# A second branch's gates by Strassen's seven products in a two-layer hybrid trunk, with the output projection's halves swapped

## The chip, the cores and the metric

One core of one Trainium2 chip runs the whole program. The metric is the time of one execution on the device in microseconds (us), the median of several runs. The engines are named as in the profile: PE is TensorE's matmuls and PEld its weight loads, DVE is VectorE, ACT is ScalarE, POOL is GpSimd, SP is the engine that issues most DMAs.

## What is computed

Two layers over 256 tokens of 1,024 features, all in fp32. The part of a layer that matters here is the mixer and its merge (`u` is the normalised input, 256 x 1024; `y_a`, `y_b`, `y_c` are the outputs of the pooling, convolution and attention branches, 256 x 512 each):

```python
u = rms_norm(h, norm_mix_g[i])
proj = u @ w_in[i]
a_in, c_x, c_b, c_c, q, k, v, gates = jnp.split(proj, split_at, axis=-1)
...
g_a, g_b, g_c = jnp.split(jax.nn.sigmoid(gates), N_BRANCHES, axis=-1)
merged = (g_a * (y_a @ w_pool_out[i])
          + g_b * (y_b @ w_conv_out[i])
          + g_c * (y_c @ w_attn_out[i]))
h = h + merged @ w_o[i]
```

Each of the three gates is a product of `u` with 1024 x 1024 columns of `w_in`. After the merge come a squared-ReLU MLP (1024 to 4096 and back) and a gated per-layer embedding.

## The kernel before

**Weights.** All weights stream from memory once, in a fixed order that `weight_plan` (line 93) writes out. A unit is 128 x 1024 fp32. `WeightStream.prefetch` (line 274) turns each unit into two parts: ScalarE rounds it to fp32r (`whi`, line 285) and VectorE subtracts that from the original (`wlo`, line 286). A product is then three matmuls: high by high, high by low, low by high. Splits run up to `AHEAD = 5` units ahead of the unit in use, in six buffers of parts. Plain loads go through three staging tiles of two units (1 MB each), issued by SP at line 250, in the order of the plan.

**Kinds of units around the change.** An A unit (`unit_a`, line 416) covers 256 rows of weights by 512 columns for both halves of the tokens: 12 matmuls of 512 columns (line 425). An S unit (`unit_s`, line 439) is half of one of Strassen's products: 6 matmuls of 512 columns (lines 444, 446, 448). A gate of 1024 x 1024 takes 8 A units, or seven products of 2 S units.

**Strassen's products.** They need sums of quarters of the weights. These are made in two tiles of 1 MB, `sums`, which come from the four-buffer pool `t8`: two plain loads by SP (line 233), one VectorE add of 128 x 2048 (line 265, after product 1 is split), and three DMAs from POOL that add to what lies there (line 256: after products 1, 5 and 6 are split). Products 1, 5, 6, 4 read the first tile, 7 the second; 2 and 3 use plain weights through the staging tiles. `sums_busy` stops all further loading at the next product 1 until product 4 is split. The token side needs four sums and differences of the input, made and split by `token_sums` (line 917) at the places in `TOKEN_SUMS_AT`.

**Sums of products.** Products 1, 6, 7, 4 add up in one bank of PSUM ("chain"), 5 and 3 in another ("five"), 2 in a third ("two"). Before the next product adds to a bank, its present content must be read out: after 1, 5 and 6 by a ScalarE copy (`copied`, line 960), after 7 by a VectorE add (line 965). VectorE adds and ScalarE sigmoids (line 970) give the four quarters of the gate. Before, this is done for branch A's gates (`GATED = 0`) and for two groups of the MLP's second product (`GROUPS`).

**The order.** `merge_order` (line 43) writes out the order of the merge: `g` are A units of a gate, `p` those of a branch's output projection, `S` a product. Side work is attached to a unit with `at(u, ...)` and emitted right after it; `u_b` is the last unit of the conv columns, so the merge starts at `u_b + 1` and has 42 units. A merge (line 996) multiplies a projection by its sigmoid (line 999) and adds it up (line 1003); when all three branches of a half of the features are in, `merge_t` transposes it (line 496) and splits it (lines 517, 518) into the operand of `w_o`. The first half is complete after `p(0, 0)`, the second after `p(0, 1)`; `w_o` (8 A units) takes the low half first. The tile framework orders each engine's instructions when it compiles, by program position and by the times that it assumes; on the chip every engine runs its list in order.

**Side work of the merge.** Attention's end, the pooling branch (windows, `pool_map`), and the convolution: `conv` (line 887) is one VectorE multiply (line 892) and two multiply-adds (line 895) for each of four groups, `conv_gate` (line 898) two multiplies and two splits.

Of the kernel before, what the change touches and what calls it, by code (L numbers as in the profile page):

```python
# [36 lines left out]
GATED = 0  # L37

TOKEN_SUMS_AT = (8, 9, 10, 12, 14, 17)
# [3 lines left out]
def merge_order():  # L43

    def g(br, f, *which):
        return [("g", br, f, ((0, 2), (4, 6))[n]) for n in which]

    def p(br, f):
        return [("p", br, f)]

    def prod(n):
        return [("S", n)]
# [40 lines left out]
def weight_plan():  # L93
# [12 lines left out]
    for i in range(DEPTH):  # L106
# [15 lines left out]
        for kind, *what in merge_order():  # L122
            if kind == "S":
                plan.extend(("S", what[0], i, k, "gate") for k in (0, 2))
# [25 lines left out]
def quarter(i, j, h, f):  # L150

    if j == "gate":
        return tuple(("A", "w_in", i, 4 * h + k, GATE + GATED * D + 512 * f) for k in (0, 2))
    return tuple(("A", "w_down", i, 4 * (j + h) + k, 512 * f) for k in (0, 2))
# [21 lines left out]
def weight_blocks():  # L176

    place = {}
    for _, block in transfer_plan():
        if block:  # L180
            place.setdefault(block, len(place))
    for i in range(DEPTH):
        for j in ("gate", *GROUPS):
            place.setdefault(quarter(i, j, 0, 1), len(place))
    return place


class WeightStream:
# [30 lines left out]
    def load(self, parts=1, between=None):  # L219


        while self.next_dma < len(self.transfers):
# [3 lines left out]
            if own and prod == 1:  # L226
# [3 lines left out]
                if j == "gate" or j == GROUPS[0]:  # L230
# [79 lines left out]
def kernel(  # L310
# [224 lines left out]
    for i in range(DEPTH):  # L535
# [344 lines left out]
        for n in range(4):  # L880
            at(u_b - 3 + n, window, n)
# [3 lines left out]
        at(u_b + 6, pool_map, 1)  # L885

        def conv(g):
# [4 lines left out]
            nc.vector.tensor_scalar_mul(out=yv[:, g, :], in0=zp[:, g, PAD:], scalar1=cw[2])  # L892
# [56 lines left out]
        def gate_product(n, k):  # L949
# [6 lines left out]
            unit_s(get(("acc", SUM[n])), *parts, n, i, k, "gate", n not in (1, 5, 2))  # L956
# [5 lines left out]
        def gate_sum(t, f, bank, n):  # L962
# [3 lines left out]
            sigmoid(t, f, v, v)  # L966

        def sigmoid(t, f, src, out):
            sig[GATED, t, f] = out
# [3 lines left out]
        def gate_product_out(n):  # L973
            gops.pop(n, None)
            if n in (1, 5):
                copied(n)
            elif n == 6:
                copied(6)
                gate_sum(0, 1, tiles.pop(("acc", "five")), 6)
            elif n == 7:  # L980
                gate_sum(1, 1, tiles[("acc", "chain")], 5)
                gops.pop(("s", 5))
            elif n == 2:
                gate_sum(0, 0, tiles.pop(("acc", "two")), 1)
            elif n == 4:
                sigmoid(1, 0, tiles.pop(("acc", "chain")), t2())

        def merge_key(br, f):
            return ("bpair", "p", br, f) if br else ("p", br, f)
# [15 lines left out]
        def merge_t(f):  # L1005
            if f == 0:
# [11 lines left out]
        for kind, *what in merge_order():  # L1018
            if kind == "S":
                for k in (0, 2):  # L1020
                    u = add(gate_product, what[0], k)
                if what[0] != 3:
                    at(u, gate_product_out, what[0])
# [342 lines left out]
```

## Time and profile before

| | before |
|---|---|
| median of 3 runs | 843.99 us (843.08 to 844.75) |
| profiled execution | 843.23 us, of which the span of the instructions is 841.4 us |
| PE busy | 834.1 us (99%) |
| DVE busy | 661.3 us (79%) |
| ACT busy | 547.6 us (65%) |
| DMA moved | 177.32 MB, mean 211 GB/s |

The profile lists for each engine its instructions with start and length; a busy share is over the span. Matmuls are pipelined: each is listed for some 0.39 us, but the next starts 0.23 us later, so their cost is read from their starts. Lengths of VectorE and ScalarE instructions also overlap a little; in a row of several alike, the whole over the count is the cost of one.

### The profile page before, as it was taken

How to read it: one execution, taken by the hardware profiler on the slowest of the kernel's cores; microseconds unless marked ns; L12 is line 12 of the kernel's file. 1: busy time of each engine (PE TensorE's matmuls, PEld its weight loads, DVE VectorE, ACT ScalarE, POOL GpSimd, SP SyncE). 2: the span in 40 equal slices, each digit the busy share in tenths (PEclk: the TensorE clock that was granted, in tenths of full speed). 3: DMA queues.
4: the chain of work that ended last, by engine and by line, in shares of the span. 5: the costliest groups of instructions: out<-in, count | busy, mean ns of one | idle time of the engine just before them, and what ended most of it. 6: DMA issues, size and time to landing. Idle time of an engine off the chain costs nothing.

```text
span 841.4 us, 11683 instructions
## 1 busy us (share of the span) xinstructions
PE 834.1 (99%) x4492; PEld 721.0 (86%) x4492; DVE 661.3 (79%) x910; ACT 547.6 (65%) x789; POOL 47.8 (6%) x52
## 2 busy tenths in 40 slices
PE   9999999999999999999999999999999999999997
PEld 7999988888988888888879998888889888888886
DVE  5987889976689677977678777998766886789864
ACT  6755566654688667976665645666546876688662
POOL 2400000000000000000022000000000000000000
PEclk9999999999999999999999999999999999999999
DMA  9864649754658766866445546486555767669531
GB/s 336 311 223 150 226 123 274 231 208 170 270 172 262 244 239 181 261 192 221 179 168 194 191 166 234 129 246 226 211 190 225 246 211 254 243 199 248 192 133 51
DMA packets 27127, 177.32 MB, mean 211 GB/s; under 512 B 3136, under 2 KB 4032, under 8 KB 6464
## 3 DMA queue, kind: packets, MB, share of 16 engines
q1 hardware_dynamic: 24192, 157.53, 50.5%
q0 software_dynamic: 2592, 18.88, 11.8%
q8 instruction: 35, 0.57, 0.3%
q10 hardware_dynamic: 288, 0.18, 0.1%
q14 instruction: 20, 0.16, 0.1%
HBM read 175.52 MB, written 1.05 MB: 210 GB/s over the span
## 4 chain that ended last, share of the span: by engine, by line
PE 98%; DMA 0%; ACT 0%; issue 0%; DVE 0%; SPq 0%
PE acc L425 38%; PE bp L473 12%; PE bp L475 6%; PE bp L425 6%; PE bp L464 5%; PE bp L462 5%; PE bp L460 5%; PE acc L446 3%; PE acc L448 3%; PE acc L444 3%; PE acc L436 3%; PE bp L448 2%; PE bp L446 2%; PE bp L444 2%; PE tr L496 1%; PE acc L1280 1%
## 5 line engine op out<-in xcount | busy, mean ns | idle before, releaser
L286 DVE TENSOR_TENSOR wlo<-stage,whi 128x1024 fp32r<-128x1024 f32 (+1 forms) x272 | 328.4, 1213 | 121.7 <-ACT whi L285 120.1
L285 ACT CAST whi<-stage 128x1024 fp32r<-128x1024 f32 (+1 forms) x272 | 282.7, 1044 | 205.4 <-PE acc L425 82.7
L425 PE MATMUL acc<-whi,t 128*128 128x512 f32 x928 | 298.7, 393 | 0.0
L425 PEld LDWEIGHTS acc<-whi,t 128*128 128x128 f32 x928 | 173.5, 188 | 35.1 <-ACT whi L285 0.4
L425 PE MATMUL acc<-wlo,t 128*128 128x512 f32 x464 | 180.9, 390 | 0.0
L473 PE MATMUL bp<-t,whi 128*128 128x512 f32 x448 | 122.3, 394 | 0.0
L425 PEld LDWEIGHTS acc<-wlo,t 128*128 128x128 f32 x464 | 87.2, 188 | 17.5 <-DVE wlo L286 0.2
L460 PE MATMUL bp<-t,whi 128*128 128x256 f32 x320 | 90.7, 284 | 0.0
L464 PE MATMUL bp<-t,wlo 128*128 128x256 f32 x320 | 90.5, 283 | 0.0
L462 PE MATMUL bp<-t,whi 128*128 128x256 f32 x320 | 90.5, 283 | 0.0
L473 PEld LDWEIGHTS bp<-t,whi 128*128 128x128 f32 x448 | 77.7, 189 | 11.3
L286 DVE TENSOR_TENSOR wlo<-t,whi 128x1024 fp32r<-128x1024 f32 x60 | 72.9, 1220 | 14.8 <-ACT whi L285 13.8
L285 ACT CAST whi<-t 128x1024 fp32r<-128x1024 f32 x60 | 62.9, 1052 | 29.1 <-PE acc L425 11.4
L475 PEld LDWEIGHTS bp<-t,wlo 128*128 128x128 f32 x448 | 68.8, 189 | 9.4
L475 PE MATMUL bp<-t,wlo 128*128 128x256 f32 x448 | 71.5, 281 | 0.0
L462 PEld LDWEIGHTS bp<-t,whi 128*128 128x128 f32 x320 | 61.1, 191 | 0.4
L460 PEld LDWEIGHTS bp<-t,whi 128*128 128x128 f32 x320 | 61.0, 191 | 0.4
L464 PEld LDWEIGHTS bp<-t,wlo 128*128 128x128 f32 x320 | 61.1, 191 | 0.1
L256 POOL DMA_DIRECT2D t<-in_w_dram x18 | 15.9, 884 | 477.4 <-ACT t L1116 192.7
L446 PE MATMUL acc<-wlo,t 128*128 128x512 f32 x104 | 40.6, 390 | 0.0
L448 PE MATMUL acc<-whi,t 128*128 128x512 f32 x104 | 40.5, 390 | 0.0
L444 PE MATMUL acc<-whi,t 128*128 128x512 f32 x104 | 40.5, 390 | 0.0
(176 smaller groups left out, 1057.9 us busy)
## 6 DMA issues: line engine op xcount, KB each, us to landing
stage<-in_w_dram SPq DMA_DIRECT2D x131, 1024.0 KB, 4.8
t<-in_w_dram POOLq DMA_DIRECT2D x18, 1024.0 KB, 8.5
t<-in_w_dram SPq DMA_DIRECT2D x12, 1024.0 KB, 6.4
stage<-in_w_dram SPq DMA_DIRECT2D x6, 512.0 KB, 5.3
stage<-in_w_dram SPq DMA_DIRECT2D x4, 256.0 KB, 4.7
h<-in_x_dram SPq DMA_DIRECT2D x4, 256.0 KB, 9.9
t<-in_xT_dram SPq DMA_DIRECT2D x1, 512.0 KB, 7.6
out_dram<-h SPq DMA_DIRECT2D x2, 256.0 KB, 2.0
```

The costliest lines, as they stand in the source:

```text
L285: self.nc.scalar.copy(out=hi[:, cs], in_=src[:, cs])
L286: self.nc.vector.tensor_sub(out=lo[:, cs], in0=src[:, cs], in1=hi[:, cs].bitcast(F32))
L425: nc.tensor.matmul(accs[t], lhsT=lhs[:, kx + j, tk], rhs=rhs[:, j, :], start=begins[t] and j == 0 and n == 0, stop=last and j == 1 and n == 2,
L436: nc.tensor.matmul(accs[half][t], lhsT=lhs[:, k, t * P:(t + 1) * P], rhs=rhs[:, 0, cs], start=k == 0 and n == 0, stop=False)
L444: nc.tensor.matmul(bank, lhsT=xh[:, k + n, :], rhs=wh[:, n, :], start=first, stop=False, skip_group_check=True)
L446: nc.tensor.matmul(bank, lhsT=xh[:, k + n, :], rhs=wl[:, n, :], start=False, stop=False, skip_group_check=True)
L448: nc.tensor.matmul(bank, lhsT=xl[:, k + n, :], rhs=wh[:, n, :], start=False, stop=k + n == 3, skip_group_check=True)
L460: nc.tensor.matmul(bp[:, m, :], lhsT=wh[:, j, ms], rhs=xh[:, kx + j, :], start=first, stop=False, skip_group_check=True)
L462: nc.tensor.matmul(bp[:, m, :], lhsT=wh[:, j, ms], rhs=xl[:, kx + j, :], start=False, stop=False, skip_group_check=True)
L464: nc.tensor.matmul(bp[:, m, :], lhsT=wl[:, j, ms], rhs=xh[:, kx + j, :], start=False, stop=last, skip_group_check=True)
L473: nc.tensor.matmul(bank, lhsT=wh[:, k, :], rhs=xk[k], start=k == 0, stop=False, skip_group_check=True)
L475: nc.tensor.matmul(bank[:, 1, :], lhsT=wl[:, k, :], rhs=xk[k][:, 0, :], start=False, stop=k == KD - 1, skip_group_check=True)
```

## The change

Branch B's gates (`g_b`) are computed by the seven products too, behind those of A and in the same two tiles of weight sums. Eight A units of B's gates per layer become fourteen S units. The token sums are made earlier, and their splits are kept until B's products have used them. The four gate units of C and the products of A now come first; `conv` and `conv_gate` move seven units back, and the first operation of `conv` moves from VectorE to ScalarE. All projections use a pair of banks of the pool `bp`. The second half of the features is now complete first, after `p(1, 1)`; the first half waits for product 4 of B, so the projection `p(1, 0)` stays in its two banks until then. `w_o` takes the high half first.

```diff
-GATED = 0
-TOKEN_SUMS_AT = (8, 9, 10, 12, 14, 17)
+GATED = (0, 1)
+TOKEN_SUMS_AT = (6, 7, 8, 9, 10, 15)
...
-    def g(br, f, *which):
-        return [("g", br, f, ((0, 2), (4, 6))[n]) for n in which]
+    def g(f, *which):
+        return [("g", 2, f, ((0, 2), (4, 6))[n]) for n in which]
...
-    order = g(2, 0, 0, 1) + g(2, 1, 0, 1) + p(2, 0) + prod(1) + p(2, 1) + prod(5) + g(1, 0, 0) + prod(3)
-    order += g(1, 0, 1) + prod(6) + p(1, 0) + prod(7) + g(1, 1, 0) + prod(2) + g(1, 1, 1) + prod(4)
-    return order + p(0, 0) + p(1, 1) + p(0, 1)
+    order = g(0, 0, 1) + prod(0, 1) + g(1, 0) + prod(0, 5) + g(1, 1) + prod(0, 3) + p(2, 0) + prod(0, 6) + p(2, 1)
+    order += prod(0, 7, 2, 4) + p(0, 0) + prod(1, 1) + p(0, 1) + prod(1, 5, 3) + p(1, 0)
+    return order + prod(1, 6, 7) + p(1, 1) + prod(1, 2, 4)
...
-        for ks in (low, high):
+        for ks in (high, low):
             for f in range(2):
                 a("w_o", ks, f * 512)
...
-                if j == "gate" or j == GROUPS[0]:
+                if j == "gate0" or j == GROUPS[0]:
                     self.sums = self.new_sums()
...
-            nc.vector.tensor_scalar_mul(out=yv[:, g, :], in0=zp[:, g, PAD:], scalar1=cw[2])
+            nc.scalar.activation(out=yv[:, g, :], in_=zp[:, g, PAD:], func=AF.Copy, scale=cw[2])
...
-            at(u_b + 15 + g, conv, g)
+            at(u_b + 22 + g, conv, g)
         for m in range(2):
-            at(u_b + 20 + m, conv_gate, m)
+            at(u_b + 27 + m, conv_gate, m)
...
-        def gate_product_out(n):
-            gops.pop(n, None)
+        def gate_product_out(br, n):
+            if br == GATED[-1]:
+                gops.pop(n, None)
...
-            return ("bpair", "p", br, f) if br else ("p", br, f)
+            return ("bpair", "p", br, f)
...
-            if f == 0:
+            if f == 1:
                 st["m"] = (t8(F32R), t8(F32R))
...
+                if what == [1, 4]:
+                    at(u, merge, 1, 0)
+                    at(u + 1, merge_t, 0)
...
-                at(u, merge, br, f)
-                if br == 0:
-                    at(u + 1, merge_t, f)
+                if (br, f) != (1, 0):
+                    at(u, merge, br, f)
+                if (br, f) == (1, 1):
+                    at(u + 1, merge_t, 1)
...
-        for ks in ((0, 2), (4, 6)):
+        for ks in ((4, 6), (0, 2)):
             for f in range(2):
-                u = add_a(("o", f), lambda: st["m"], "w_o", ks, f * 512)
-                if ks[0]:
+                for k in ks:
+                    u = add(lambda f=f, k=k: unit_a(get(("o", f)), *st["m"], "w_o", i, k, f * 512, k, k == 4, k == 2))
+                if not ks[0]:
                     at(u, residual, f)
```

The other lines of the diff pass the branch's number on to the functions of the products.

## Rows read from the trace of the kernel before

**Rows 1.** The page, part 1: busy time, share of the span, instructions.

```profile
PE 834.1 (99%) x4492; PEld 721.0 (86%) x4492; DVE 661.3 (79%) x910; ACT 547.6 (65%) x789; POOL 47.8 (6%) x52
```

**Rows 2.** The page, part 4: the chain that ended last, by engine.

```profile
PE 98%; DMA 0%; ACT 0%; issue 0%; DVE 0%; SPq 0%
```

**Rows 3.** Stretches: us; busy of PE, PEld, DVE, ACT, POOL; clock, DMA share, GB/s.

```profile
92.50:194.50 102.00, 102.00 (x481) 85.10 (x480) 88.59 (x127) 64.54 (x83) 4.83 (x5) 1.00 0.63 203
111.00:157.00 46.00, 46.00 (x209) 38.05 (x209) 45.55 (x61) 30.37 (x39) 2.81 (x3) 1.00 0.72 206
194.50:221.00 26.50, 26.50 (x128) 22.03 (x127) 17.68 (x22) 13.94 (x21) 0.00 (x0) 1.00 0.58 216
```

**Rows 4.** The chain in order of time: start, length, a run of two A units.

```profile
136.47 5.44 PE acc L425 x24
```

**Rows 5.** Timeline of PE: start, length, line, operation, tiles, shape, count.

```profile
85.71 0.39 PE L716 MATMUL acc<-t,qT 128*128 128x512 f32 x1
...
122.70 0.39 PE L444 MATMUL acc<-whi,t 128*128 128x512 f32 x1
122.93 0.39 PE L425 MATMUL bp<-whi,t 128*128 128x512 f32 x1
...
133.59 0.39 PE L444 MATMUL acc<-whi,t 128*128 128x512 f32 x1
...
136.08 0.39 PE L448 MATMUL acc<-whi,t 128*128 128x512 f32 x1
136.31 0.39 PE L425 MATMUL acc<-whi,t 128*128 128x512 f32 x1
...
200.50 1.04 PE L496 MATMUL tr<-csb,t 128*128 128x128 f32 x8
```

**Rows 6.** Timeline of DVE; in brackets the idle time before, and what ended it.

```profile
110.15 1.23 DVE L286 TENSOR_TENSOR wlo<-stage,whi 128x1024 fp32r<-128x1024 f32 x1 [2.23 <-ACT whi L285]
...
118.92 2.28 DVE L265 TENSOR_TENSOR t<-t,t 128x2048 f32<-128x2048 f32 x1
...
126.84 2.35 DVE L286 TENSOR_TENSOR wlo<-t,whi 128x1024 fp32r<-128x1024 f32 x2
...
133.19 1.13 DVE L892 TENSOR_SCALAR t<-t,par 128x256 f32<-128x256 f32 x4
...
135.98 1.28 DVE L999 TENSOR_TENSOR t<-bp,t 128x512 f32<-128x512 f32 x2
137.18 1.66 DVE L895 SCALAR_TENSOR_TENSOR t<-t,par,t 128x256 f32<-128x256 f32 x4
...
194.09 1.28 DVE L999 TENSOR_TENSOR t<-acc,t 128x512 f32<-128x512 f32 x2
195.29 1.28 DVE L1003 TENSOR_TENSOR t<-t,t 128x512 f32<-128x512 f32 x2
...
202.24 1.28 DVE L518 TENSOR_TENSOR t<-tr,t 128x512 fp32r<-128x512 f32 x2
```

**Rows 7.** Timeline of ACT.

```profile
110.59 0.48 ACT L486 ACTIVATE t<-tr,par 128x256 fp32r<-128x256 f32 x1
...
136.50 0.59 ACT L960 COPY t<-acc 128x512 f32<-128x512 f32 x1 [0.26 <-PE acc L448]
...
201.25 1.07 ACT L517 CAST t<-tr 128x512 fp32r<-128x512 f32 x2 [0.19 <-PE tr L496]
```

**Rows 8.** Line 256, the adding DMAs: ns of issue min/median/max, and landing.

```profile
L256 POOL DMA_DIRECT2D t<-in_w_dram x18: 865/872/1056, 121.9 to 771.4; - x18
...
DMA to landing us min/median/max: 7.9/8.5/9.4
```

**Rows 9.** Line 233, the first loads of the weight sums: landing.

```profile
DMA to landing us min/median/max: 4.7/6.4/9.7
```

**Rows 10.** Timeline of SP's DMA issues: start, length, line, count.

```profile
85.95 0.80 SPq L233 DMA_DIRECT2D t<-in_w_dram  x2
```

**Rows 11.** The page, part 3: POOL's DMA queue, packets, MB, share of 16 engines.

```profile
q0 software_dynamic: 2592, 18.88, 11.8%
```

More of the change, by code (lines that the diff above doesn't have):

```diff
@@ L123, in weight_plan @@
             if kind == "S":
-                plan.extend(("S", what[0], i, k, "gate") for k in (0, 2))
+                plan.extend(("S", what[1], i, k, f"gate{what[0]}") for k in (0, 2))
             elif kind == "g":
@@ L150, in quarter @@
 def quarter(i, j, h, f):
-    if j == "gate":
-        return tuple(("A", "w_in", i, 4 * h + k, GATE + GATED * D + 512 * f) for k in (0, 2))
+    if isinstance(j, str):
+        return tuple(("A", "w_in", i, 4 * h + k, GATE + int(j[4:]) * D + 512 * f) for k in (0, 2))
     return tuple(("A", "w_down", i, 4 * (j + h) + k, 512 * f) for k in (0, 2))
@@ L182, in weight_blocks @@
     for i in range(DEPTH):
-        for j in ("gate", *GROUPS):
+        for j in (*(f"gate{br}" for br in GATED), *GROUPS):
             place.setdefault(quarter(i, j, 0, 1), len(place))
@@ L884 @@
         at(u_b + 5, pool_map, 0)
[L885 removed]
+        at(u_b + 5 + 1, pool_map, 1)
         def conv(g):
@@ L955, in gate_product @@
                 parts = gops[n]
-            unit_s(get(("acc", SUM[n])), *parts, n, i, k, "gate", n not in (1, 5, 2))
+            unit_s(get(("acc", SUM[n])), *parts, n, i, k, f"gate{br}", n not in (1, 5, 2))
         def copied(n):
@@ L960, in copied, with gate_sum @@
             nc.scalar.copy(out=s_, in_=tiles[("acc", SUM[n])])
-        def gate_sum(t, f, bank, n):
+        def gate_sum(br, t, f, bank, n):
             s_ = gops.pop(("s", n)) if n != 5 else gops["s", n]
@@ L965, in gate_sum, with sigmoid @@
             nc.vector.tensor_add(out=v, in0=bank, in1=s_)
-            sigmoid(t, f, v, v)
-        def sigmoid(t, f, src, out):
-            sig[GATED, t, f] = out
+            sigmoid(br, t, f, v, v)
+        def sigmoid(br, t, f, src, out):
+            sig[br, t, f] = out
             nc.scalar.activation(out=out, in_=src, func=AF.Sigmoid,
                                  scale=st["nrstd" if f else "rstd"][:, t:t + 1])
-        def gate_product_out(n):
-            gops.pop(n, None)
+        def gate_product_out(br, n):
+            if br == GATED[-1]:
+                gops.pop(n, None)
             if n in (1, 5):
@@ L978, in gate_product_out @@
                 copied(6)
-                gate_sum(0, 1, tiles.pop(("acc", "five")), 6)
+                gate_sum(br, 0, 1, tiles.pop(("acc", "five")), 6)
             elif n == 7:
-                gate_sum(1, 1, tiles[("acc", "chain")], 5)
+                gate_sum(br, 1, 1, tiles[("acc", "chain")], 5)
                 gops.pop(("s", 5))
             elif n == 2:
-                gate_sum(0, 0, tiles.pop(("acc", "two")), 1)
+                gate_sum(br, 0, 0, tiles.pop(("acc", "two")), 1)
             elif n == 4:
-                sigmoid(1, 0, tiles.pop(("acc", "chain")), t2())
+                sigmoid(br, 1, 0, tiles.pop(("acc", "chain")), t2())
         def merge_key(br, f):
-            return ("bpair", "p", br, f) if br else ("p", br, f)
+            return ("bpair", "p", br, f)
         def gate(br, f):
@@ L1020 @@
                 for k in (0, 2):
-                    u = add(gate_product, what[0], k)
-                if what[0] != 3:
-                    at(u, gate_product_out, what[0])
+                    u = add(gate_product, *what, k)
+                if what[1] != 3:
+                    at(u, gate_product_out, *what)
+                if what == [1, 4]:
+                    at(u, merge, 1, 0)
+                    at(u + 1, merge_t, 0)
             elif kind == "g":
```

8 lines of the change are left out of this document (4 added, 4 removed).

## The prediction

> **What bounds the kernel now.** I read the page first: PE is busy for 99% of the span, DVE for 79%, ACT for 65% [rows 1]. A busy PE need not be the bound, so the chain that ended last comes next: 98% of it is PE, and nothing else has a share of a per cent [rows 2]. Then the merge, where the change lies, by stretches: in layer 0 from 92.5 to 194.5 us, the start of the merge to that of `w_o`, PE is busy throughout at full granted clock, and in the 46 us from 111 to 157 it stays so although DVE has only 0.45 us of idle time [rows 3]. So PE bounds the kernel, and the five units of splits ahead bridge a DVE that is full for a while. Two things follow: work taken from PE shortens the span one for one, and DVE, busy for 88.59 of the 102 us [rows 3], is next in line.
>
> **The change part by part.**
>
> *Matmuls.* Two A units run for 5.44 us, so one is 2.72 us [rows 4]. One whole product takes from 133.59 to 136.31 us, so an S unit is 1.36 us [rows 5]. Per layer 8 A units go (21.76 us) and 14 S units come (19.04 us): 2.72 us less, 5.44 us in both layers. The order of projections and the halves of `w_o` move no matmul in or out.
>
> *VectorE.* Its costs by steps [rows 6]: a split is 1.12 us (two take 2.35, a single one 1.23); an operation on 128x512 is 0.60 us (two from 135.98 to 137.18); a multiply-add of `conv` 0.41, its multiply 0.28, the add of the weight sums 2.28. Per layer come six splits (6.7), one more add (2.3) and three sums of products (1.8), and four multiplies go (1.1): 9.7 us more. The merge of the first half (four operations, 2.4 us) moves behind the last product, beside `w_o`, where DVE is busy 17.68 of 26.5 us [rows 3]. What is left is 88.6 + 9.7 - 2.4 = 95.9 us of DVE in a merge of 102 - 2.7 = 99.3 us. That fits, with 3 us to spare.
>
> Whether it fits at each place is another question. The worst is from product 7 of A to product 5 of B: 14 units, 10 of them S, so 13.6 + 10.9 = 24.5 us on PE. DVE has there 14 splits (15.7), the multiply-adds of `conv` (3.3), `conv_gate` (2.4), two sums (1.2), the add of the weight sums (2.3) and the two merges of branch A (4.8): 29.7 us. It loses 5.2 us, 4.6 of its lead of five splits. PE comes out just covered, with some 0.5 us of lead. I take nothing for it; the end of the range is that DVE also stands idle there, as for 2.23 us at 110 us [rows 6].
>
> *Waits on a bank.* This is what the new order adds. In A's products other units lie between a product whose bank is read out and the next that adds to it. In B, product 3 follows 5 at once, and 7 follows 6 at once. The read-out has a row: product 5's last matmul starts at 136.08 and PE goes on at 136.31 [rows 5]; the copy runs from 136.50 to 137.09 [rows 7]. A next product on the same bank would stand for 137.09 - 136.31 = 0.8 us. Below, the cost is nothing: the compiled order fills holes, as the S matmul at 122.70 in the middle of a projection shows [rows 5]. To fill it PE needs the third unit ahead split. Behind product 5 the lead is used up, so I take 0.8 us there, nearest to the row. Behind product 6 DVE has won back 3.6 us (10.9 us of PE against six splits and a sum, 7.3), so `p(1, 1)` fills that hole: nothing. Two layers: 1.6 us.
>
> *The turn to `w_o`.* Its cover was a projection and four units; now the second half has the two last products, 5.4 us. The chain: two multiplies and two adds, 2.4 us [rows 6], transposes 1.0 [rows 5], then the casts from 201.25 and the subtractions, the first done at 202.9 [rows 6, 7], 1.4 us after the transposes. That is 4.8 us, covered if the transposes are put between the products. In the trace of before they stand at 200.50, 3.9 us after the adds were done at 196.57 [rows 5, 6]. Put behind the last product, they would leave PE waiting 1.4 us per layer. I take nothing and keep 1.4.
>
> *ScalarE.* Six casts, three copies and four 128x256 operations at 0.48 [rows 7], some 10 us, on 64.54 of 102 us [rows 3]: hidden; without that cover the copy above would be late too. One such late cast is the end of the bound, about 1 us.
>
> *DMAs.* SP issues as many loads as before per layer: four plain ones become two plain and two of weight sums. POOL issues three more adding ones, 0.87 us each of a queue that is idle, landing in 8.5 us, at most 9.4 [rows 8]. A's first loads move three transfers forward in SP's queue, where they wait, with all loads behind them, for the tiles of the keys: the last score matmul is at 85.71 us [rows 5], the loads go at 85.95 [rows 10] in both orders. They land within 9.7 us [rows 9], and PE comes to the product after 103 us: covered. B's first load waits for the split of A's product 4. From then PE has six S and two A units, 13.6 us, against a split, 9.7 us of landing at worst and a split [rows 6, 9], 12 us: covered, with 1.6 us to spare.
>
> *Buffers.* The products of B need no further tile, and the token splits are kept longer in a pool of 17, of which I count 16 in use: no wait. The operand of `w_o` takes the tiles of the weight sums, the second of them once product 4 of B is split, five units ahead.
>
> The sum: 843.23 - 5.44 + 1.6 = 839.4 us against the profiled execution, which lies 0.76 us under the median; against the median 840.2 us.
>
> **The rivals.**
>
> *The full gain.* Every hole is filled, as all holes before were: 843.99 - 5.44 = 838.6 us. For it speaks a PE without a gap beside a full DVE [rows 3]; against it that no product before stood right behind another on its bank.
>
> *All three waits are paid.* Both bank waits and the turn to `w_o`: 0.8 + 0.8 + 1.4 = 3.0 us per layer, 838.6 + 6.0 = 844.6 us, no change. For it speak the late transposes [rows 5, 6]; against it the row at 122.70.
>
> *VectorE becomes the bound.* In the stretch from A's product 7 to B's product 5 only 0.5 us of lead is left by my sum. Every us beyond that in which DVE waits there for a cast, a landing or a bank goes to PE, and the splits behind it are late. Two idle times like the one of 2.23 us make 4.5 - 0.5 = 4.0 us per layer: 838.6 + 8.0 = 846.6 us, slower. It decides the sign from 4.1 us of idle time in that stretch. Against it: while full, DVE lost only 0.45 of 46 us [rows 3]. The bank waits would hide beneath it.
>
> *The adding DMAs come late.* Between the two splits of B's product 6 and the first of product 4 lie the adding DMA of the second sum; from the end of unit 34 to the start of 47 PE has 21.8 us. DVE up to 5.2 us late, two splits (2.5), two casts (2), 0.9 of issue and 8.5 of landing make 19.1, so it hurts once landings pass 11.2 us. POOL's 18 took 11.8% of 841.4 us, 5.5 us each of all 16 engines [rows 11]; three more raise the merge's 0.63 [rows 3] to an estimated 0.81. Landings twice as long would cost 5.8 us per layer: 850.2 us. Against it: the longest landing is 9.4 us and the longest issue 1.06, with a stretch of 0.72 DMA share and a full DVE among them [rows 3, 8]. The Trainium skill (SBUF — State Buffer, section "SBUF: two separate sides") has a rule that speaks for this rival: a DMA from POOL's queue starves while VectorE runs an operation that uses both read ports for one tensor, and the page gives 620 ns becoming some 3,100. By its factor of five the issue of 0.87 us would take 3.5 us more, an estimate, 0.8 beyond the room of 2.7, and the sum would be 841.8. No issue in this trace is stretched so.
>
> **How the numbers follow.** The forecast has a chance of 0.33, the full gain 0.31, the paid waits in part or whole 0.18 (a quarter of it below 842.3), VectorE as bound 0.12, late DMAs 0.06. A measurement of this kernel can tell about 0.2% from no change, 1.7 us: faster ends at 842.3, slower begins at 845.7. Faster: 0.33 + 0.31 + 0.05 = 0.69. Slower: 0.12 + 0.06, less what of them stays small, 0.16. Same: 0.15. The range runs from 0.8 us below the full gain (the spread of the runs of before), 837.8, to 845.6, past the paid waits; it leaves out most of the last two rivals.
>
> **What would show it.** PE's instructions fall from 4492 to 4468. After B's product 5 PE should have a gap of about 0.8 us that ends on the copy of line 960, one in each layer, and none after product 6 or before `w_o`; with no gap the full gain is right. DVE in the merge should be full from A's product 7 on, with PE waiting on no `wlo`. A PE that waits for `wlo` there proves VectorE the bound; a split of product 4 that waits for POOL's DMA proves the last rival. The forecast is wrong if PE loses more than 3 us in a merge, or if a gap appears outside of it.

## The result, and the profile after the change

The changed kernel takes 865.06 us (median of 4 runs, 864.64 to 866.06) against 843.92 us for the kernel before in the same session: ratio 1.0255, interval 1.0243 to 1.0267. That is 21 us slower; the forecast was 840.2 us, with 845.6 as the end of its range. The profiled execution took 864.64 us, its span 862.8 us, 21.4 more than before.

The page of the changed kernel, parts 1, 4 and 5:

```profile
PE 835.8 (97%) x4468; PEld 718.3 (83%) x4468; DVE 679.0 (79%) x922; ACT 561.4 (65%) x815; POOL 53.2 (6%) x58
...
PE 26%; DVE 1%; DMA 1%; issue 0%; ACT 0%; ACTq 0%
...
L285 ACT CAST whi<-t 128x1024 fp32r<-128x1024 f32 x80 | 82.7, 1049 | 50.7 <-DMA t<-in_w_dram 27.8
```

PE has the 24 instructions fewer that the sum wanted, and is busy for 97% where it was 99% [rows 1]. The chain that ended last is no longer PE alone: where 98% was PE [rows 2], the chain could be followed on PE for only 26%. The third row is the first hint of the cause: ScalarE's casts of weight sums (`t`, not `stage`) had 50.7 us of idle time before them, 27.8 of it ended by a DMA.

The stretches of [rows 3], and one more, of layer 0 (columns as there):

```profile
92.50:194.50 102.00, 94.99 (x433) 77.68 (x432) 86.53 (x117) 65.16 (x84) 7.57 (x8) 0.98 0.72 212
111.00:157.00 46.00, 45.06 (x204) 37.11 (x203) 42.64 (x57) 33.40 (x46) 1.43 (x2) 1.00 0.75 233
177.50:186.00 8.50, 4.24 (x11) 2.85 (x10) 4.62 (x5) 5.69 (x7) 0.86 (x1) 0.80 0.64 223
194.50:221.00 26.50, 22.68 (x106) 18.21 (x105) 21.04 (x25) 13.48 (x17) 0.00 (x0) 1.00 0.53 194
```

PE stands idle for 7.0 us of the merge and 3.8 us of the turn to `w_o`; both were full. The third row holds the worst place. What PE waited for from 92.5 to 221 us, line by line (us in total, times, longest):

```profile
PE acc L444 <- ACT whi L285: 3.5, 1, 3.5
PE acc L425 <- DVE t L518: 1.9, 1, 1.9
PE tr L496 <- DVE t L1004: 1.6, 1, 1.6
PE acc L444 <- DVE t L798: 1.1, 1, 1.1
PE acc L444 <- DVE t L965: 0.9, 1, 0.9
PE acc L446 <- DVE wlo L286: 0.8, 1, 0.8
PE acc L444 <- ACT t L960: 0.7, 1, 0.7
PE acc L425 <- ACT t L517: 0.3, 1, 0.3
```

PE's timeline gives each its place and its price: the distance of two starts, less the 0.23 us of a matmul at full clock.

```profile
169.90 0.50 PE L444 MATMUL acc<-whi,t 128*128 128x512 f32 x1 [0.68 <-ACT t L960]
...
177.51 0.39 PE L425 MATMUL bp<-whi,t 128*128 128x512 f32 x1
181.40 0.51 PE L444 MATMUL acc<-whi,t 128*128 128x512 f32 x1 [3.50 <-ACT whi L285]
182.66 0.79 PE L446 MATMUL acc<-wlo,t 128*128 128x512 f32 x1 [0.76 <-DVE wlo L286]
183.26 0.63 PE L448 MATMUL acc<-whi,t 128*128 128x512 f32 x1
183.68 0.63 PE L444 MATMUL acc<-whi,t 128*128 128x512 f32 x1
...
202.40 0.87 PE L496 MATMUL tr<-csb,t 128*128 128x128 f32 x6 [1.60 <-DVE t L1004]
203.62 0.50 PE L425 MATMUL acc<-whi,t 128*128 128x512 f32 x1 [0.35 <-ACT t L517]
...
207.61 0.97 PE L425 MATMUL acc<-whi,t 128*128 128x512 f32 x3 [1.87 <-DVE t L518]
```

- At 181.40 B's product 6 begins, 3.66 us late, then loses 1.03 and 0.36 more, and the next matmuls start 0.43 us apart where 0.23 is usual, until 186.1: 1.3 us. Together 6.3 us, and 5.5 in layer 1.
- The turn to `w_o` loses 1.77, 0.51 and 2.03 us: 4.3, and 4.1 in layer 1.
- Product 3 of B behind 5, at 169.90: 0.84 us in each layer.
- A's product 1, on an accumulator bank that attention's last scaling (line 798) still reads: 1.3 and 0.7. A's product 4 behind 7, on the sum of line 965: 1.1 and 0.9.
- Behind five of the waits in each layer the first two matmuls start 0.30 to 0.34 us apart, as at 169.90 and 170.24 us, and not 0.23: 0.5 us per layer.

The sum is 13.8 + 12.0 + 1.0 = 26.9 us. Less the 5.44 us of matmuls saved it leaves 21.4, as by the spans: the saving came in full, and losses of five times its size stand against it, all of them in the two merges and the turns to `w_o`. The change of layers lost nothing. PE has short waits there, but the kernel before had the same; the rows are before's (421 us) and the changed kernel's (433 us):

```profile
421.34 0.41 PE L496 MATMUL tr<-csb,h 128*128 128x128 f32 x2 [0.48 <-DVE h L1252]
...
432.82 0.41 PE L496 MATMUL tr<-csb,h 128*128 128x128 f32 x2 [0.47 <-DVE h L1258]
```

**The chain to product 6.** Four views of the changed kernel, first VectorE's timeline: the split that ends A's use of the first tile, the split of B's product 1, the add of the weight sums, the split of product 6.

```profile
148.02 1.21 DVE L286 TENSOR_TENSOR wlo<-t,whi 128x1024 fp32r<-128x1024 f32 x1
...
155.30 2.36 DVE L286 TENSOR_TENSOR wlo<-t,whi 128x1024 fp32r<-128x1024 f32 x2 [2.60 <-ACT whi L285]
...
159.31 2.28 DVE L265 TENSOR_TENSOR t<-t,t 128x2048 f32<-128x2048 f32 x1
...
181.38 1.23 DVE L286 TENSOR_TENSOR wlo<-t,whi 128x1024 fp32r<-128x1024 f32 x1 [7.64 <-ACT whi L285]
```

POOL's timeline, the adding DMAs into the second and the first tile:

```profile
162.13 0.86 POOL L256 DMA_DIRECT2D t<-in_w_dram  x1 [28.35 <-ACT t L960]
167.10 0.86 POOL L256 DMA_DIRECT2D t<-in_w_dram  x1 [4.10 <-DVE wlo L286]
```

Their landing, line 256 in a window around each of the two, in that order, and over the whole span:

```profile
DMA to landing us min/median/max: 9.1/9.1/9.1
...
DMA to landing us min/median/max: 13.1/13.1/13.1
...
L256 POOL DMA_DIRECT2D t<-in_w_dram x24: 862/865/1056, 101.7 to 792.7; - x24
...
DMA to landing us min/median/max: 7.7/8.6/13.1
```

And ScalarE's timeline, which stands idle until the second of them has landed:

```profile
169.26 0.59 ACT L960 COPY t<-acc 128x512 f32<-128x512 f32 x1 [1.78 <-PE acc L448]
180.31 3.89 ACT L285 CAST whi<-t 128x1024 fp32r<-128x1024 f32 x4 [10.46 <-DMA t<-in_w_dram]
```

Read it as one line. A's product 4 is split at 149.2; B's first load goes out at 149.26 and lands 4.9 us later; product 1 is split by 157.7; the add ends at 161.6; one adding DMA leaves at 162.13, the next at 167.10 behind product 5's split, and lands at 180.23 because it is the second of the two; product 6 can be split at 180.31. From A's split to B's that is 31 us. PE has less to do in that time: from 149.89, when A's product 4 starts, it has product 4, a projection, product 1, a projection, products 5 and 3 and a projection, that is 4 x 2.72 + 3 x 5.44 = 27.2 us. A lead of five units would cover the difference, but VectorE had hardly any left at 149 us. The kernel before showed little of the line: its 18 adding DMAs landed within 9.4 us [rows 8], and the closest of them were issued 7.8 and 7.9 us apart (121.92 and 129.76 us, and the same place in layer 1), where the second landed in 8.2 and 9.0 us.

### The profile page after: what moved, and what is told of

Its sections match the earlier page's. It is cut to its first block, busy times and chain, and to the rows that moved or that the text cites. A ratio compares the mean times of both kernels' runs of the same rounds, so it can differ in the third digit from the quotient of the medians.

```text
span 862.8 us, 11697 instructions
## 1 busy us (share of the span) xinstructions
PE 835.8 (97%) x4468; PEld 718.3 (83%) x4468; DVE 679.0 (79%) x922; ACT 561.4 (65%) x815; POOL 53.2 (6%) x58
## 5 line engine op out<-in xcount | busy, mean ns | idle before, releaser
L286 DVE TENSOR_TENSOR wlo<-stage,whi 128x1024 fp32r<-128x1024 f32 (+1 forms) x264 | 318.0, 1212 | 99.6 <-ACT whi L285 98.3
L285 ACT CAST whi<-stage 128x1024 fp32r<-128x1024 f32 (+1 forms) x264 | 272.7, 1043 | 170.6 <-PE acc L425 78.4
L425 PE MATMUL acc<-whi,t 128*128 128x512 f32 x736 | 237.4, 394 | 4.4 <-DVE t L518 3.7
L425 PEld LDWEIGHTS acc<-whi,t 128*128 128x128 f32 x736 | 137.4, 188 | 33.1 <-DVE t L518 4.6
L425 PE MATMUL acc<-wlo,t 128*128 128x512 f32 x368 | 143.4, 390 | 0.0
L286 DVE TENSOR_TENSOR wlo<-t,whi 128x1024 fp32r<-128x1024 f32 x80 | 96.4, 1220 | 36.7 <-ACT whi L285 35.3
L285 ACT CAST whi<-t 128x1024 fp32r<-128x1024 f32 x80 | 82.7, 1049 | 50.7 <-DMA t<-in_w_dram 27.8
L425 PEld LDWEIGHTS acc<-wlo,t 128*128 128x128 f32 x368 | 69.2, 188 | 13.7
L444 PE MATMUL acc<-whi,t 128*128 128x512 f32 x160 | 63.8, 401 | 10.8 <-ACT whi L285 6.1
L446 PE MATMUL acc<-wlo,t 128*128 128x512 f32 x160 | 64.2, 401 | 1.5 <-DVE wlo L286 1.5
L448 PE MATMUL acc<-whi,t 128*128 128x512 f32 x160 | 63.6, 398 | 0.0
L425 PE MATMUL bp<-whi,t 128*128 128x512 f32 x192 | 61.1, 389 | 0.0
```

What stands on the lines that cost most here:

```text
L285: self.nc.scalar.copy(out=hi[:, cs], in_=src[:, cs])
L286: self.nc.vector.tensor_sub(out=lo[:, cs], in0=src[:, cs], in1=hi[:, cs].bitcast(F32))
L425: nc.tensor.matmul(accs[t], lhsT=lhs[:, kx + j, tk], rhs=rhs[:, j, :], start=begins[t] and j == 0 and n == 0, stop=last and j == 1 and n == 2,
L444: nc.tensor.matmul(bank, lhsT=xh[:, k + n, :], rhs=wh[:, n, :], start=first, stop=False, skip_group_check=True)
L446: nc.tensor.matmul(bank, lhsT=xh[:, k + n, :], rhs=wl[:, n, :], start=False, stop=False, skip_group_check=True)
L448: nc.tensor.matmul(bank, lhsT=xl[:, k + n, :], rhs=wh[:, n, :], start=False, stop=k + n == 3, skip_group_check=True)
```

## The experiments

All ratios are to the kernel before, in runs of the same session. Line numbers in rows of experiments are those of the kernel that was run.

**Without B's adding DMAs** (`add_to` is not called for B's gates):

```diff
+        if j == "gate1" and prod in (5, 6):
+            return
...
-            self.add_to(snd, i, j, 1, 1)
+            if j != "gate1":
+                self.add_to(snd, i, j, 1, 1)
```

> Leaves out the three adding DMAs of branch B's weight sums in each layer, so B's sums are incomplete; all matmuls, splits and loads stay. Theory (the chain through the first tile of weight sums is too long for the units between): B's product 6 no longer waits (3.5 us of gap, 1.0 for its low part and the half clock behind it, some 6 us per layer), and VectorE, which stood idle for 7.6 us there, comes to the turn to w_o earlier: 865 us falls to between 845 and 854. Rival (VectorE is the bound): its work is the same, so the time stays within 2 us of 865.

Measured: 850.38 us, ratio 1.0081 (1.0052 to 1.0110). The wait at product 6 is gone in both layers, and 14.7 us with it. What stays in layer 0 is the bank waits (1.3, 1.1, 0.6) and 3.05 us at the turn: those are not this chain's.

**With less for VectorE** (the convolution's multiply-adds and its gating left out):

> Leaves out the convolution's eight multiply-adds and two gating multiplies on VectorE in each layer, some 4.5 us of its work per layer; DMAs and matmuls stay. Theory (chain through the weight sums): the wait before B's product 6 stays within 1 us of 3.5, the time falls by 3 us at most (862 to 866). Rival (VectorE is the bound): every us taken from VectorE comes out, 9 us in two layers: about 856.

Measured: 863.73 us, 1.0239 (1.0209 to 1.0269). Product 6 waits as before (3.5 and 1.0 us), though A's product 4 is now split at 145.9, 3.3 us earlier: B's first load took 6.3 us instead of 4.9 and the pair of adding DMAs, from 159.66 to 178.53, 18.9 instead of 18.1. Two bank waits went, others came (at the transposes before `w_o` 2.5 us in place of 1.8). VectorE's load is not what makes the change slow.

**The adding DMAs exchanged in the program:**

> Issues B's adding DMA of the second tile (needed for product 7) behind that of the first after product 5 (needed for product 6); nothing is left out. Theory: the first tile's adding DMA lands 8.6 us after its issue instead of 13.1, product 6 starts some 4.5 us earlier in each layer and keeps the clock, product 7 is not later than now: 6 to 10 us less in all, 855 to 859. Rival (VectorE is the bound): nothing changes, 865. A second rival (the transfers are slow because of other loads, not of each other): the landing stays at 12 to 13 us and so does the time.

Measured: 866.98 us, 1.0278 (1.0248 to 1.0308). The compiled order on POOL was the old one, with the two DMAs again 4.96 us apart and the second landing after 13.2 us: the run says nothing on the question.

**The adding DMAs in two halves each:**

> Each adding DMA of the gates' weight sums is issued as two of 512 KB, one for each unit; nothing is left out. Theory: the first half lands earlier, product 6's first unit can be split some 4 us sooner: 4 to 8 us less in all, 857 to 861. If an adding DMA costs a fixed time whatever its size, the queue gets longer and the time rises by 4 us or more. Rival (VectorE is the bound): nothing changes.

Measured: 879.66 us, 1.0428 (1.0398 to 1.0458), 15 us slower, in the range of the second possibility. A half alone took 5.5 us, so the time is not the same whatever the size, but it is more than half of a whole one's. In layer 0 the first four halves of B land after 5.5 to 16.4 us, at 172.3, 178.1, 183.2 and 188.1: one behind the other, 21.4 us from the first issue to the last landing where the two whole ones took 18.1. Halves of 512 KB are no way round the line. PE also waits longer for VectorE, in both layers together 5.7 us at A's product 1 (1.7 in the changed kernel) and 6.3 at the transposes before `w_o` (3.0); why wasn't followed up.

**The order on POOL forced** (the first tile's before the second's, behind product 5's split):

```diff
-            self.add_to(snd, i, j, 1, 1)
+            if j != "gate1":
+                self.add_to(snd, i, j, 1, 1)
...
-            self.add_to(fst, i, j, 1, 1)
+            first = self.add_to(fst, i, j, 1, 1)
+            if j == "gate1":
+                with self.tc.issue_after(first.ins):
+                    self.add_to(snd, i, j, 1, 1)
```

> Only the order of B's two adding DMAs on POOL is turned round: the one into the first weight-sum tile (which product 6 splits) goes out before the one into the second (which product 7 splits). Nothing is left out, no transfer more or less. Theory (product 6 of B waits because its adding DMA lies in line behind the other): the first tile's adding DMA lands about 8.6 us after its issue and not 13.1, so product 6 begins some 4.5 us earlier per layer, its wait (4.7 and 3.8 us) and the matmuls at half clock behind it (2 and 1.2 us) go, and the time falls by 10 to 12 us to 853 to 856. Rival (the landing is long whatever goes before it, the amount of data decides): the first tile's adding DMA still lands 12 us or more after its issue, and the time stays at 863 to 867. A third possibility is that the wait moves on to product 7, which then has the late tile: then 857 to 862.

Measured: 870.66 us, 1.0320 (1.0304 to 1.0335). Landing of the two DMAs of layer 0, and PE's timeline behind product 6:

```profile
DMA to landing us min/median/max: 8.4/12.4/16.3
```

```profile
181.14 0.39 PE L453 MATMUL acc<-whi,t 128*128 128x512 f32 x1
187.80 1.22 PE L430 MATMUL bp<-whi,t 128*128 128x512 f32 x2 [6.28 <-ACT whi L290]
```

Issued 0.5 us apart, the first lands after 8.4 us and the second after 16.3: whichever is second takes half as long again or twice as long. Counted from the landing of the first, the second takes 8.5 us here (176.3 to 184.7) and 9.0 in the changed kernel (171.3 to 180.2), about one landing of its own: the two went one after the other. Product 6 no longer waits; what follows it does, for 6.28 us, because ScalarE must first cast product 7, whose tile now lands last. The third possibility was right in kind and too cheap by 9 us: issuing both late wastes the 5 us by which one could go ahead. From the first issue to the last landing the pair takes 16.8 us here and 18.1 in the changed kernel, in either order.

**Plain DMAs in place of the adding ones**, same bytes, queue and places:

```diff
-        self.nc.gpsimd.dma_start(out=t, in_=..., accum_op=ALU.add)
+        op = {} if j == "gate1" else {"accum_op": ALU.add}
+        self.nc.gpsimd.dma_start(out=t, in_=..., **op)
```

> B's three DMAs per layer that add to a weight-sum tile move the same bytes through the same queue at the same places, but overwrite the tile instead of adding to it (left out: the additions, so B's products use other weights). Theory (it is the adding that makes them long and puts them in line): each lands 5 to 7 us after its issue, the first tile's not after 13; the wait at B's product 6 goes as when these DMAs are left out altogether (850.4 us): 849 to 853. Rival (the POOL queue or the bytes beside the weight stream set the landing): they land after 8 and 12 to 13 us as before, and the time stays at 862 to 866.

Measured: 851.52 us, 1.0086 (1.0070 to 1.0101). The three of layer 0, and the stretch where the changed kernel had its wait:

```profile
L257 POOL DMA_DIRECT2D t<-in_w_dram x3: 527/538/558, 163.7 to 178.1; - x3
...
DMA to landing us min/median/max: 5.0/5.1/5.6
```

```profile
177.50:186.00 8.50, 8.50 (x40) 7.02 (x39) 7.69 (x8) 6.73 (x8) 0.53 (x1) 1.00 0.77 271
```

They land after 5.0 to 5.6 us, so that the first of the pair is through when the second leaves. PE is full where it stood for half the time. So neither the bytes nor POOL's queue make these DMAs long, but the adding: 13.5 us of the change's time (865.06 - 851.52) hang on it, 14 by the two ratios.

**Blocks moved on PE.** The first run moves one projection block from A to B, between products 5 and 3:

> Only one block of matmuls (the first half of the third branch's projection, 2 units, 5.4 us) is moved: from ahead of A's product 6 to between B's products 5 and 3. Nothing is left out. Theory (B's chain of load, sum, adding DMA and split is too long by 4 to 5 us for the matmuls that stand beside it, while A's has time to spare): B's wait at product 6 (4.7 and 3.8 us, with 2 and 1.2 us of slow matmuls) and the bank wait between products 5 and 3 (0.84 per layer) go, A gets no new wait, and the time falls by 11 to 13.5 us to 851.5 to 854. Rival (A's chain is as tight, since the adding DMAs take as long there): the wait comes back ahead of A's product 6, and the time is 860 to 866.

Measured: 863.64 us, 1.0239 (1.0222 to 1.0256), the rival's time. Not its reason, though: product 6 waits less (1.7 us, and as much in the projection behind it), but A's product 4 now waits 2.8 us on its bank in both layers, product 3 of B still 2.9 in layer 1, and the turn 3.8 and 3.7.

The next moves a block from between A's products 6 and 7 to behind A's product 4, so that B's chain has 5.4 us more of matmuls beside it:

> One block of matmuls alone is moved (the second half of the third branch's projection, 2 units, 5.4 us): from between A's products 6 and 7 to behind A's product 4. Nothing is left out, and B's part of the order is as in the changed kernel. Theory (B's chain starts when A's product 4 is split and is 4 to 6 us too long): the split of A's product 4, and with it B's first load, both adding DMAs and the split of product 6, come 5.4 us earlier against product 6, its waits (4.7 and 3.8 us) and the half-clock matmuls behind them go, and the time falls by 9 to 12 us to 853 to 856; the bank waits and those at the turn to w_o stay. Rival (the chain is set by what VectorE and POOL do between A's product 4 and B's product 5, not by its start): product 6 still waits 3 us or more, and the time is 861 to 865.

Measured: 872.63 us, 1.0340 (1.0321 to 1.0359), outside both. ScalarE's and PE's timelines at A's product 7, and the stretch behind it:

```profile
141.49 1.04 ACT L285 CAST whi<-t 128x1024 fp32r<-128x1024 f32 x1 [4.71 <-DMA t<-in_w_dram]
142.44 0.58 ACT L960 COPY t<-acc 128x512 f32<-128x512 f32 x1
```

```profile
143.08 0.80 PE L444 MATMUL acc<-whi,t 128*128 128x512 f32 x1 [4.67 <-ACT t L960]
```

```profile
143.00:148.00 5.00, 4.92 (x12) 3.91 (x13) 3.73 (x5) 3.05 (x5) 0.00 (x0) 0.50 0.92 326
```

Now A's own adding DMA, the one behind product 6 (issued at 133.44, landing 8.0 us later), stands in the way: ScalarE comes to the cast of product 4 before it has landed, waits 4.71 us, and the copy that frees PE's bank is queued behind that cast. So a late weight sum stops not just its product but everything that ScalarE does. B's product 6 still waits 2.9 us as well, near the rival's 3. More room for B's chain was taken from A's, which has adding DMAs of 8 us too.

Three more orders go the same way; the first two times lie above everything expected. Both moves together, with the new order of the next paragraph:

> Nothing left out. The order of the run with the new order of blocks (858.6 us), with A's product 4 ahead of the second half of the third branch's projection as well. Theory: what that run had left at B's product 6 (5.9 us in the first layer, 5.5 in the second, with the slow matmuls) goes too: 846 to 849. Rival (a new wait in A, where products 6, 7, 2 and 4 now stand without a block between them and product 4 needs the adding DMA behind product 6): 851 to 857.

Measured: 865.53 us, 1.0253 (1.0237 to 1.0270). Waits on line 960 and on `wlo` at A's products (0.9, 2.0, 1.5 us), then 2.5 at B's product 6.

> Nothing left out. As the run that moves the one block behind A's product 4, and the second branch's first projection block stands between B's products 5 and 3 and not between 3 and 6; only one block is left between B's product 7 and its last two products, as in the changed kernel. Theory: the waits at product 6 go and the bank wait between 5 and 3 gives way to one of about 0.9 between 3 and 6; the waits at the turn (4.3 us per layer) stay, since they need the second block: 853 to 856. Rival (the turn's waits come from the late product 6 and its pile of work, and go with it): 845 to 849.

Measured: 866.35 us, 1.0267 (1.0250 to 1.0284). A's product 7 waits 4.3 us on line 960; the turn keeps its 4.2 in layer 0.

> Nothing left out. As the run before it, but A's products 1 and 5 stand one block of the third branch's gate later. Theory: the wait for an accumulator bank at A's product 1 (1.3 and 0.6 us) goes and the rest stays: 1 to 2 us below the run before it. Rival (A's own chain from product 5's split to product 6 becomes too short, since both adding DMAs then stand closer together): 2 to 6 us above it.

Measured: 880.55 us, 1.0429 (1.0408 to 1.0451). The wait at A's product 1 gave way to one of 3.7 us, of C's gate for the sigmoid (line 995) that frees its bank; the loss against the run before is 14 us, not the rival's 2 to 6.

**A new order of blocks** that fills the hole between B's products 5 and 3 and puts two blocks ahead of B's last two products:

```diff
-    ... prod(0, 3) + p(2, 0) + prod(0, 6) + p(2, 1)
-    order += prod(0, 7, 2, 4) + p(0, 0) + prod(1, 1) + p(0, 1) + prod(1, 5, 3) + p(1, 0)
-    return order + prod(1, 6, 7) + p(1, 1) + prod(1, 2, 4)
+    ... prod(0, 3, 6, 2, 7) + p(2, 1)
+    order += prod(0, 4) + p(0, 0) + prod(1, 1) + p(0, 1) + prod(1, 5) + p(2, 0) + prod(1, 3)
+    return order + prod(1, 6, 7) + p(1, 1) + p(1, 0) + prod(1, 2, 4)
```

> Only the order of the blocks is changed, nothing is left out: the stretch between B's product 1 and product 6 keeps its length, but a projection's block stands between products 5 and 3 and not 3 and 6, and two blocks (10.9 us) stand after B's product 7 and ahead of its products 2 and 4. Theory: the bank wait between products 5 and 3 of B (0.84 us per layer) goes, the wait at product 6 stays (4.7 and 3.8 us and the slow matmuls), and the waits at the turn to w_o (4.3 us per layer) shrink only if they come from VectorE's work piled up behind B's late products; then the time falls by some 6 to 10 us to 855 to 859. Rival (the turn's waits come from the last products' own fold alone, which takes as long in any order): the time falls by 2 us at most, 863 to 865.

Measured: 858.64 us, 1.0176 (1.0151 to 1.0201), as expected. PE's timeline at the turn:

```profile
198.79 1.03 PE L496 MATMUL tr<-csb,t 128*128 128x128 f32 x8
```

The eight transposes run without a gap, and `w_o` follows without one. The hole behind product 5 is gone, product 6's wait stays (2.4 and 3.1 us, with half-clock matmuls behind it), and 0.9 us each is new between A's products 3 and 6 (line 960) and in A's next product (line 518). With the forced order on POOL on top:

> The new order of blocks and the turned order of B's adding DMAs together. Theory: the two savings lie at different places and add: 865 less 10 to 12 for product 6 and less 2 to 10 for the bank wait and the turn, so 843 to 853. Rival (the stretch is bound by something else, such as VectorE's total, as soon as one wait is gone): no better than the better of the two alone, 853 to 856.

Measured: 864.94 us, 1.0240 (1.0219 to 1.0261): worse by 6 us and above both expectations, for the wait behind product 6 is 4.9 and 5.4 us, as in the forced run.

**A third tile.** B's first quarter gets a tile of its own, so its load need not wait for A's product 4. The room comes from small buffers, so there is a control without the third tile:

```diff
+                elif j == "gate1":
+                    self.sums = (self.third(), self.sums[1])
...
+        if prod == 7 and j == "gate0":
+            self.sums_busy = False
...
-    u8 = ctx.enter_context(tc.tile_pool(name="u8", bufs=4))
+    u8 = ctx.enter_context(tc.tile_pool(name="u8", bufs=5))
...
-    u2 = ctx.enter_context(tc.tile_pool(name="u2", bufs=17))
+    u2 = ctx.enter_context(tc.tile_pool(name="u2", bufs=15))
```

> The changed kernel with 15 instead of 17 buffers of the pool of 2 KB tiles: the control for the two runs that need this room for a third weight-sum tile. Nothing left out. If those two buffers have slack: 864 to 867; if not, this run's excess over 865 is to be taken off the other two.

> B's first quarter goes into a third weight-sum tile, and B's two first loads may go out when A's product 7 is split instead of when its product 4 is. Nothing left out; two 2 KB buffers fewer. Theory (B's chain starts with the release of A's first tile and is a few us longer than the matmuls beside it): the first load is issued some 7 us earlier, the split of B's product 1 is no longer held up by it (2.6 us on VectorE's queue), and all behind it comes 3 us or more earlier: product 6's wait falls from 4.7 and 3.8 us to under 2 and the half-clock matmuls go, 6 to 10 us in all: 855 to 859. Rival (the split of product 1 comes no earlier, because VectorE's queue holds it): as the control, within 2 us.

Measured: the control 871.54 us, 1.0326 (1.0288 to 1.0365), so the two buffers had no slack; with the third tile 857.88 us, 1.0162 (1.0147 to 1.0177), inside what was expected. Against its control, whose four runs spread from 868.75 to 875.28 us, the tile is worth 13.7 us: the framework moved the load of B's first quarter to where the tile is free, 15.6 us in layer 0, so that only the splits, the add and the adding DMAs are left of the chain. PE's waits from 92.5 to 221 us:

```profile
PE tr L503 <- DVE t L1011: 2.9, 1, 2.9
PE bp L432 <- DVE wlo L292: 2.8, 2, 1.6
PE acc L453 <- DVE wlo L292: 0.7, 1, 0.7
PE acc L432 <- ACT t L524: 0.3, 1, 0.3
```

The second adding DMA still takes 13.2 us to land, but at 175.0, and product 6 waits 0.9 us for it. The rest of the waits are VectorE's, but for one. With the new order:

> The third tile with the new order of blocks that alone gave 858.6 us. Theory: the waits at product 6 that were left there (5.9 and 5.5 us with the slow matmuls) shrink as in the run before this one: 848 to 853. Rival: no gain over 858.6, or a loss as with the other moves of A's blocks (865).

Measured: 862.42 us, 1.0221 (1.0202 to 1.0240), the rival: ScalarE's copy (line 960) is late at A's products (1.1 and 3.3 us in layer 0) and in layer 1 also at B's (6.7 us). Then the room was taken from other buffers:

> As the run with the third weight-sum tile (857.9 us), but its room is taken elsewhere: 16 buffers of 2 KB tiles instead of 15, and 2 of the smallest instead of 4. Nothing left out. Theory (the missing small buffers cost that run what they cost its control, some 6 us): 852 to 856. Rival (they cost it nothing, since its waits now are VectorE's): 856 to 859.

Measured: 855.87 us, 1.0147 (1.0130 to 1.0164). It lies at the border of the two expectations and does not decide between them. It is the fastest version here that leaves nothing out, and 12 us behind the kernel before. The same with the light convolution:

> The run before it with the convolution's multiply-adds and its gating multiplications left out (eight and two VectorE instructions per layer, as in the first light run; its output differs in these). Theory (with the chain of B's weight sums cured, VectorE is what is late next: the four waits that remain per layer all end on VectorE): 5 to 9 us below the run before it. Rival (they end on the chain still): within 2 us of it, as the light run was of the changed kernel.

Measured: 854.30 us, 1.0129 (1.0114 to 1.0144), 1.6 us less: the rival's number. The two longest of PE's waits from 92.5 to 221 us, by this run:

```profile
PE acc L451 <- ACT whi L291: 2.4, 1, 2.4
PE tr L503 <- DVE t L1006: 1.8, 1, 1.8
```

VectorE's waits shrink, and a wait for a cast of weight sums comes back: both limits lie at about the same place, and taking one away uncovers the other.

## Why the prediction was wrong

**Matmuls and splits.** Right: 4468 instructions, and the spans fit with 5.44 us saved. VectorE was full from 116 to 152 us. That its lead would be nearly used up was right, but the prediction had it fall from A's product 7 to B's product 5, and it fell earlier: the two units of A's product 4 are split by 146.9 and 149.2 us, and without its bank wait PE would have come to them at 148.8 and 150.2. One to two us were left there.

**The step that failed** is the paragraph on the DMAs, by two errors. First, it counted from the split of A's product 4 "six S and two A units, 13.6 us" up to B's product 1. That is the distance with all five units of lead in hand. The paragraph on VectorE spends 4.6 of them on the way to B's product 5, and in the run the second unit was split 1 us before PE came to it. Second, it stopped at product 1. The chain goes on through the add and two adding DMAs to product 6, and I gave each of these DMAs its own landing of 8.5 us; only the link from product 6 to product 4 was worked out. The rows of before could not show what a pair 5 us apart does: with the same four units between the two, theirs left 7.8 us apart. B's left 5.0 us apart because VectorE had no lead: it waited 2.60 us for product 1's casts, and the splits up to product 5's then followed as fast as it could make them. An estimate tells the two errors apart: with the median landing of 8.6 us the tile would have been there at 175.7 us, and PE came to product 6 at 177.7, so without the second error the first would have cost little or nothing there. The run with the third tile shows the converse: the landing is still 13.2 us, but the chain starts earlier, and product 6 waits 0.9 us.

**The rival of late adding DMAs** (0.06, 850.2 us) named the right resource at the wrong link, and decided from landings beyond 11.2 us; 13.1 and 12.3 were measured, in one pair per layer. Its sign, a split of product 4 that waits for POOL's DMA, is there as well (ScalarE's cast at 191.91 us, 1.13 us), but PE does not wait for it. Without the wait at product 6 the time is 850 us, so the rest of the loss is not its. Its sentence on the Trainium skill's rule (SBUF — State Buffer, section "SBUF: two separate sides") was not put to the test: the issues of line 256 take 862 to 1056 ns in the changed kernel, as before, and beside those of B's DMAs VectorE runs splits, which take two tensors each. The longest issue of any run is 1.24 us, of one DMA right behind another. Nor does VectorE explain the late DMA: it was idle from 173.7 us until after the landing at 180.23.

**Bank waits.** B's 5 to 3 was taken at 0.8 and measured 0.84, ending on line 960 as said; 6 to 7 cost nothing, and for the reason given: `p(1, 1)` stands in the hole (from 186.81 us), and also in the run without B's adding DMAs, where product 6 is not late. Not seen: A's product 1 behind line 798 (2.0 us in both layers) and product 4 behind 7 (2.0). The first comes from A's products moving ahead of the other gates, up against attention's end, which I priced for loads and not for banks; with A's product 1 one block later, in the last of the three orders, it is gone.

**The turn to `w_o`** was taken at nothing with 1.4 as its end. It measured 4.3 us in layer 0, 3.05 of it also when product 6 no longer waits. VectorE's timeline of the changed kernel shows where the bound was short:

```profile
202.27 2.35 DVE L286 TENSOR_TENSOR wlo<-stage,whi 128x1024 fp32r<-128x1024 f32 x2
204.54 0.68 DVE L1000 TENSOR_TENSOR t<-bp,t 128x512 f32<-128x512 f32 x1
205.14 1.21 DVE L286 TENSOR_TENSOR wlo<-stage,whi 128x1024 fp32r<-128x1024 f32 x1
206.27 0.68 DVE L1000 TENSOR_TENSOR t<-bp,t 128x512 f32<-128x512 f32 x1
206.87 1.27 DVE L518 TENSOR_TENSOR t<-tr,t 128x512 fp32r<-128x512 f32 x2
```

The subtractions that `w_o` needs are the last row; three splits and the other half's multiplies lie ahead of them in VectorE's queue. The bound had summed the chain alone, as if the engine had nothing else to do. Two blocks of matmuls ahead of the last products hide it all.

**VectorE as the bound** (846.6 us) fell as the first cause (863.7 us with ten instructions per layer left out) and is one of two limits once the chain is cured.

**What stays open:** why VectorE is so much later with the adding DMAs in halves, and whether any order of blocks brings the change level; the fourteen runs above that leave nothing out took 855.9 to 880.6 us.

## What to carry to other kernels

Follow a chain that is fed by a reused buffer from the release of the buffer to the last use that depends on it, with the lead that is really left there, and put each transfer of a kind behind the one that is still under way. When work is moved closer together, ask which transfers now overlap for longer than any did in the trace at hand, since their durations there are nearly those of a transfer alone. A late transfer also stops what is queued behind the instruction that waits for it: here one cast on ScalarE held the copy that freed PE's bank.

## What the runs showed of the hardware

- An adding DMA of 1 MB landed 7.7 to 9.4 us after its issue in the changed kernel, but 13.1 and 12.3 us where another had been issued 5 us earlier, and 16.3 (forced order) where another had been issued 0.5 us earlier: 8.1 to 9.0 us after the other's landing in each of the three. Plain DMAs of the same bytes at the same places on the same queue took 5.0 to 5.6 us, with 0.54 instead of 0.86 us of issue.
- Behind waits of 3.5 and 0.76 us (changed kernel, 177.5 to 182.7) matmuls ran 0.43 us apart for 2.6 us, and behind one of 4.67 us the granted clock of the next 5 us was 0.50, the lower level of 1.2 GHz. Waiting costs PE once in standing and again in the matmuls that follow: 1.3 of the 6.3 us at product 6.
